# A one-core decode step: four order changes, compression weights loaded at once, and pinned loads

## The chip, the cores and the metric

The kernel runs on one core of one Trainium2 chip. The metric is device time in microseconds of one execution, as the median of several runs; lower is better. PE is the matmul engine (PEld its weight loads), DVE the vector engine, ACT the scalar engine, POOL the third elementwise engine, which also issues the gathers, and SP the engine whose queue issues most DMA transfers.

## The reference

One layer of a decoder step for a prompt of 1024 new tokens and 8 sample tokens that stand behind 2048 cached ones. D = 1024, 8 heads of 64, 2 key/value heads.

```python
h = rms_norm(x, norm_g)
proj = h @ w_in              # b, c gates, conv input, z_conv, q, kv (3 branches), gate logits, z_attn
q, k: rms_norm per head, rope
kv_cmp = compress_blocks(kv, cmp_pe, cmp_w)   # einsum('bcrjgd,rjde->bcjge'), blocks of 32 rows
o = gate0 * attn(q, kv_cmp) + gate1 * attn(q, top-16 blocks of 64) + gate2 * attn(q, last 512)
conv = short_conv(b * conv_in) * c
mix = concat(conv * silu(z_conv), o * silu(z_attn))
y = x + mix @ w_out
```

For the sample tokens the compressed branch covers the paged cache: its rows are gathered by the page table and multiplied by the compression weights cmp_w. All values are float32.

## The kernel before

Every large product is made of three matmuls on a high and a low part of each operand (h*h, l*h, h*l): a `copy` on ACT rounds a tile to its high part (L78), and a `sub` on DVE or POOL (L82) makes the low part. Each such pair of a copy and a subtraction stands between a tile's arrival and the matmuls that read it.

The program is written as Python generators, "streams". `merge` (L31) takes from the stream that is behind by its own costs; a stream says with `yield c` that it issued work of cost c. A tile framework then reorders the instructions of each engine by its own cost model, unless `keep` (keep_in_program_order) or `issue_after` binds them. Each engine carries out its own list in order, so an instruction that waits holds up all behind it on that engine.

The first merge runs `phase0` (norm, key/value rows, queries) beside the channel products. The second runs `first` (attention, then `out_stream`, the output projection by tiles of 128 tokens and 512 columns) beside `second` (convolution, `prefetch`, `early_out`, `cmp_stream`, `sample_stream`). The stages that the change touches:

- `kv_tile` and the compression of the prompt's rows: for pairs of key/value tiles, `token_pairs` (L427) loads rows across into `pr` with four DMAs, and `cmp_transposes` (L435, matmuls at L440) turns them. It is posted some steps later, as given at L657.
- The queries: `q_tile` runs twice with two sets of weights. The second set's four pieces are fetched by `w_loader`'s `fetch` (L169, DMA L171) and split by `split` (ACT L78, then POOL or DVE L82) between the tiles (L783 to L788). `tok_mm` does the products (L210 to L212), and `norm_rope` (L256) normalises and rotates the queries (DVE L267 to L277).
- `prefetch` (L1542) loads eight w_out pieces, which an earlier stage has split into DRAM (`wo_d`), fetches the compression weights cmp_w for the sample in four pieces (`cw_fetch`, L447; four DMAs each, L454) into one room, each with a copy and a subtraction, and issues the first two gathers of cached rows (`gather`, L1124, DMA L1127; two rooms `raw`). `early_out` (L1593) makes two output tiles early, while the attention ends.
- `cmp_stream` (L1131) has 16 units n. Each takes one gathered tile, regroups it with four copies (`regroup`, L1135, two on ACT and two on POOL), turns four pairs by PE (L1149), splits each into xh and xl, and multiplies by the compression weights (`product`, L1170), CD pairs behind. Its output goes into accs. `out_stream` runs beside it, at L1582 to L1588.
- `sample_stream` (L1301) does the sample's attention. The state rows `sdw`, `sd` come by SP (L1238), the gathered rows by POOL. In `values` (L1438), p is turned, `ptz` gets its high part from ACT and its low part from DVE, and the matmuls `o<-vhl,ptz` (L1466) follow. At the end, for two halves h, the sums are scaled (L1504 to L1514) and turned (L1515, `ptx`); from them come `mS` and the sample's own output rows (L1617).

```python
if rows is not None and t < 8:      # L656
    posts.append((lambda pr=token_pairs(rows, t - 1), t=t: cmp_transposes(pr, t - 1), 4 if t < 5 else 3 if t < 7 else 1))
if t in (3, 4, 5):                  # L787
    nxt[2](t - 2, ACT, EL)
raw = wpool.tile([128, 4, 2, 64], F32, name="cwr", tag="wx" if wpool is wk else "cwr")         # L449
r = rawp.tile([128, 2048], F32, name="raw", bufs=2)                                            # L1126
```

## Time and profile before

| what | value |
|---|---|
| median of 3 runs | 920.47 us (914.07 to 924.98) |
| the profiled execution, its own time | 922.36 us |
| span in its profile | 920.6 us |
| mean granted clock of PE | 0.978 |
| PE busy | 874.4 us, 95% |
| DVE, ACT, POOL busy | 63%, 58%, 44% |

The span goes from the first to the last instruction in the profile. An engine is busy while it carries out an instruction; a bracket behind a row of the timeline, as [2.33 <-DVE rb L275], says how long the engine stood idle just ahead and what it last waited for. PEclk is the share of the full 2.4 GHz that PE was granted.

### The profile page before, as it was taken

How to read it: one execution, taken by the hardware profiler on the slowest of the kernel's cores; microseconds unless marked ns; L12 is line 12 of the kernel's file. 1: busy time of each engine (PE TensorE's matmuls, PEld its weight loads, DVE VectorE, ACT ScalarE, POOL GpSimd, SP SyncE). 2: the span in 40 equal slices, each digit the busy share in tenths (PEclk: the TensorE clock that was granted, in tenths of full speed). 3: DMA queues.
4: the chain of work that ended last, by engine and by line, in shares of the span. 5: the costliest groups of instructions: out<-in, count | busy, mean ns of one | idle time of the engine just before them, and what ended most of it. 6: DMA issues, size and time to landing. Idle time of an engine off the chain costs nothing.

```text
span 920.6 us, 16583 instructions
## 1 busy us (share of the span) xinstructions
PE 874.4 (95%) x5769; PEld 784.8 (85%) x5769; DVE 576.8 (63%) x1482; ACT 532.7 (58%) x1350; POOL 400.5 (44%) x547
## 2 busy tenths in 40 slices
PE   8998999999899999999989999999989999999987
PEld 6898999989789889899979898999878788677765
DVE  5865627776555555765685677657745555765663
ACT  5552425433665655666565755666756776777761
POOL 4231303111454444544353543444654444677751
PEclk9998989989899999999999999999989999999999
DMA  7432402620011001220111000000977552667611
GB/s 261 127 96 71 120 10 77 223 80 21 16 30 36 24 24 46 70 69 13 59 58 24 24 12 13 24 1 7 274 263 270 198 193 94 239 214 245 221 67 48
DMA packets 67154, 91.14 MB, mean 99 GB/s; under 512 B 19191, under 2 KB 49343, under 8 KB 64894
## 3 DMA queue, kind: packets, MB, share of 16 engines
q1 hardware_dynamic: 58428, 52.16, 18.5%
q0 software_dynamic: 8064, 37.75, 12.3%
q8 instruction: 46, 0.75, 0.3%
q14 instruction: 38, 0.31, 0.1%
q10 hardware_dynamic: 578, 0.17, 0.1%
HBM read 77.92 MB, written 15.29 MB: 101 GB/s over the span
## 4 chain that ended last, share of the span: by engine, by line
PE 47%; ACT 7%; DVE 7%; issue 3%; POOL 3%; DMA 2%; SPq 0%; ACTq 0%; DVEq 0%; POOLq 0%
PE o L1024 7%; PE pt L1014 5%; PE s L940 5%; PE mm L227 5%; PE mm L225 5%; PE mm L226 5%; POOL P L989 2%; PE om L1170 2%; ACT P L930 1%; PE mm L1582 1%; PE mm L1583 1%; PE o L1466 1%; PE mm L1584 1%; PE pt L1149 1%; ACT ph L78 1%
## 5 line engine op out<-in xcount | busy, mean ns | idle before, releaser
L225 PE MATMUL mm<-hH,wh 128*128 128x384 f32 (+1 forms) x480 | 157.6, 328 | 2.3 <-ACT mixC L397 1.3
L227 PE MATMUL mm<-hH,wl 128*128 128x384 f32 (+1 forms) x480 | 154.9, 323 | 0.1
L226 PE MATMUL mm<-hL,wh 128*128 128x384 f32 (+1 forms) x480 | 154.6, 322 | 0.0
L82 POOL TENSOR_TENSOR wl<-wraw,wh 128x256 fp32r<-128x256 f32 (+1 forms) x105 | 78.1, 761 | 142.2 <-ACT wh L78 119.2
L930 ACT ACTIVATE P<-P,stat 128x640 f32<-128x640 f32 (+7 forms) x192 | 113.0, 590 | 38.1 <-DVE stat L928 37.5
L82 DVE TENSOR_TENSOR pl<-pt,ph 128x512 fp32r<-128x512 f32 (+1 forms) x164 | 102.8, 636 | 50.6 <-ACT ph L78 49.3
L78 ACT ACTIVATE ph<-pt 128x512 fp32r<-128x512 f32 (+1 forms) x164 | 88.4, 548 | 68.9 <-PE pt L1014 68.1
L989 POOL TENSOR_SCALAR P<-P,stat,gates 128x640 f32<-128x640 f32 (+7 forms) x128 | 100.3, 793 | 55.2 <-DVE stat L980 52.1
L1014 PE MATMUL pt<-ident,P 128*128 128x128 f32 x592 | 95.3, 279 | 6.1 <-POOL P L989 3.7
L940 PE MATMUL s<-k,q 128*128 128x320 f32 (+8 forms) x416 | 95.8, 333 | 1.9 <-DVE stat L928 1.9
L210 PE MATMUL mm<-wh,hH 128*128 128x256 f32 (+1 forms) x320 | 95.6, 299 | 1.3 <-ACT hH L78 0.7
L211 PE MATMUL mm<-wl,hH 128*128 128x256 f32 (+1 forms) x320 | 95.2, 297 | 1.7 <-DVE wl L82 0.9
L212 PE MATMUL mm<-wh,hL 128*128 128x256 f32 (+1 forms) x320 | 94.9, 296 | 1.2 <-DVE hL L82 1.2
L225 PEld LDWEIGHTS mm<-hH,wh 128*128 128x128 f32 x480 | 91.0, 190 | 3.3 <-ACT mixC L397 1.5
L227 PEld LDWEIGHTS mm<-hH,wl 128*128 128x128 f32 x480 | 91.3, 190 | 0.5 <-POOL wl L82 0.5
L226 PEld LDWEIGHTS mm<-hL,wh 128*128 128x128 f32 x480 | 91.3, 190 | 0.2
L928 DVE CUSTOM_DVE_ANT_0 P<-s,mask 128x32 f32<-128x32 f32 (+8 forms) x160 | 70.8, 473 | 26.2 <-PE s L940 22.3
L1014 PEld LDWEIGHTS pt<-ident,P 128*128 128x128 f32 x592 | 70.3, 140 | 19.3 <-POOL P L989 10.2
L1024 PE MATMUL o<-ph,v 128*128 128x256 f32 x264 | 74.5, 301 | 2.2 <-ACT ph L78 1.6
L1024 PE MATMUL o<-pl,v 128*128 128x256 f32 x264 | 73.4, 300 | 1.6 <-DVE pl L82 1.5
L940 PEld LDWEIGHTS s<-k,q 128*128 128x128 f32 x416 | 66.5, 190 | 6.1 <-PE pt L1014 1.6
L210 PEld LDWEIGHTS mm<-wh,hH 128*128 128x128 f32 x320 | 64.4, 201 | 2.4 <-ACT hH L78 1.4
(385 smaller groups left out, 2064.9 us busy)
## 6 DMA issues: line engine op xcount, KB each, us to landing
wraw<-in_w_in_dram SPq DMA_DIRECT2D x54, 256.0 KB
wo<-wo_d POOLq DMA_DIRECT2D x8, 512.0 KB, 5.7
out_s_win_dram<-in_state_win_kv_dram SPq DMA_DIRECT2D x8, 511.0 KB
xr<-in_x_prompt_dram SPq DMA_DIRECT2D x14, 256.0 KB
out_y_prompt_dram<-xr SPq DMA_DIRECT2D x14, 256.0 KB
sd<-in_state_win_kv_dram SPq DMA_DIRECT2D x5, 512.0 KB
mixA<-in_x_prompt_dram SPq DMA_DIRECT2D x4, 512.0 KB
xt<-in_x_prompt_dram SPq DMA_DIRECT2D x4, 512.0 KB
```

What stands on the lines that cost most here:

```text
L78: return ACT.activation(out, in_, AF.Copy)
L82: return eng.tensor_tensor(out, a, b, OP.subtract)
L210: PE.matmul(o[:, :n], hH[t // 3][:, k, s], wh, start=k == 0, stop=False)
L211: PE.matmul(o[:, :n], hH[t // 3][:, k, s], wl, start=False, stop=False)
L225: PE.matmul(o[:, :n], wh, hH[c][:, k], start=k == 0, stop=False)
L226: PE.matmul(o[:, :n], wh, hL[c][:, k], start=False, stop=False)
L227: PE.matmul(o[:, :n], wl, hH[c][:, k], start=False, stop=k == 7)
L930: return lambda: ACT.activation(P, P, AF.Exp, bias=stt[:, 0, c:c + 1], scale=-1.0, accum_out=stt[:, 1, c:c + 1])
L940: PE.matmul(s[:, a:b], q[:, i], k, start=first, stop=not first)
L989: POOL.tensor_scalar(P[:, i, :n], P[:, i, :n], stt[:, 2, c + i:c + i + 1], gates[:, qi, gt:gt + 1], op0=OP.mult, op1=OP.mult)
L1014: PE.transpose(p[:, y * 256 + i * 128:y * 256 + i * 128 + 128], src[:, i], ident)
L1024: PE.matmul(o[0][:, :256], v, X[:, y * 256:y * 256 + 256], start=br == 1 and x == 0 and y == 0 and X is h[0], stop=last and y + 1 == len(p ...
```

## The change

- A: the transposes of the last pair of tokens are posted two steps later instead of one.
- B: the fourth piece of the second query weights is fetched at t = 5 into one of two rooms named `rows`, and split at t = 7; before it went into a `wraw` room at t = 2 and was split at t = 5.
- C: the four pieces of cmp_w for the sample are fetched all at once into one tile that takes one of the two `raw` rooms; their copies stand among the steps of the early output tiles, in program order on ACT. The first gather is issued in `prefetch`, the second behind the fourth copy.
- D: the products run three pairs behind instead of two; regroup of the next unit comes half a unit later; the steps of `sample_start` are bound behind what was issued before them on ACT, DVE and POOL.
- E: the first half's end, `ends(0)`, is issued after the last low half of ptz.
- The second four w_out pieces (k of 4 and above) keep program order on SP and ACT; loads of state rows are issued after the store of the latest output tile.

```diff
+    def behind(*engines):
+        traced = nc.cur_bb.bb.instructions
+        with ExitStack() as st:
+            for e in engines:
+                st.enter_context(tc.issue_after(next(i for i in reversed(traced) if i.engine == e.engine)))
+            yield
...
-                r = home.tile([128, kp, n], F32, name=name, bufs=raw_bufs if name == "wraw" else 1)
+                if name == "rows":
+                    r = home.tile([128, 512], F32, name=name, bufs=ROWS).rearrange("p (k n) -> p k n", k=kp)
+                else:
+                    r = home.tile([128, kp, n], F32, name=name, bufs=raw_bufs if name == "wraw" else 1)
...
-            copy(ACT, h, raw)
+            r = copy(ACT, h, raw)
+            if not early:
+                keep(r)
...
-                posts.append((lambda pr=token_pairs(rows, t - 1), t=t: cmp_transposes(pr, t - 1), 4 if t < 5 else 3 if t < 7 else 1))
+                posts.append((lambda pr=token_pairs(rows, t - 1), t=t: cmp_transposes(pr, t - 1), 4 if t < 5 else 3 if t < 7 else 2))
...
+                    if t == 5:
+                        nxt[1](3, wk, "rows")
                     if t == 2:
                         nxt[2](0, ACT, EL)
-                        nxt[1](3)
-                    if t in (3, 4, 5):
-                        nxt[2](t - 2, ACT, EL)
+                    if t in (3, 4, 7):
+                        nxt[2]({3: 1, 4: 2, 7: 3}[t], ACT, EL)
...
-    CD = 2
+    CD = 3
...
-            if n + 1 < 16:
-                regroup(n + 1)
             if n in (4, 7, 10):
-                next(start, None)
+                with behind(ACT, DVE, POOL):
+                    next(start, None)
...
             for j in range(2):
+                if j and n + 1 < 16:
+                    regroup(n + 1)
...
-            SP.dma_start(r, state_win[b].rearrange("(p s) c -> p (s c)", s=4))
+            with tc.issue_after(stored[0].ins):
+                SP.dma_start(r, state_win[b].rearrange("(p s) c -> p (s c)", s=4))
...
-            sub(DVE, pz[:, :, 4:32:9, :], pv, f(pz[:, :, 0:28:9, :]))
+            last[0] = sub(DVE, pz[:, :, 4:32:9, :], pv, f(pz[:, :, 0:28:9, :]))
...
-        for h in range(2):
+        def ends(h):
...
+        with tc.issue_after(last[0].ins):
+            ends(0)
+        ends(1)
...
-        SP.dma_start(r, w_out[:, k, n * 512:(n + 1) * 512])
+        d = SP.dma_start(r, w_out[:, k, n * 512:(n + 1) * 512])
+        if k >= 4:
+            keep(d)
...
-            copy(ACT, w[:, 0], r)
+            c = copy(ACT, w[:, 0], r)
+            if k >= 4:
+                keep(c)
...
-        late = None
+        raw = rawp.tile([128, 4, 4, 2, 64], F32, name="raw", bufs=2)
+        for i in range(4):
+            cw_late.append(cw_fetch(raw[:, i], i))
...
-            if k % 2 == 0:
-                if late:
-                    late(cw2)
-                late = cw_fetch(rawp, k // 2)
             yield PREF
-        for i in range(2):
-            gather(i)
-            yield PREF
-        late(cw2)
-        yield 0
+        gather(0)
+        yield PREF
...
+        o = 0
         for t, homes in enumerate((("20", "00", "01", "10", "11"), ("11", "21", "00", "01", "10"))):
             homes = [f"q{i}" for i in homes]
-            yield from out_tile(0, t, lambda name, dt: qkv.tile([128, 512], dt, name=homes.pop(0)))
+            for c in out_tile(0, t, lambda name, dt: qkv.tile([128, 512], dt, name=homes.pop(0))):
+                yield c
+                if c and (t or o):
+                    cw_late.pop(0)(cw2)
+                o = c
+        cw_late.pop(0)(cw2)
+        gather(1)
```

The lines of the changed kernel are shifted: L78 is L88 there, L82 is L92, L1587 is L1615.

On DVE, in the query stage (B), the list before reads as follows; wl is the low half of a weight piece, from the room that stands behind the arrow, kd a piece of w_out that is split into DRAM, and q, qn, rs, ss, rb belong to the norm and the rotation of a query tile.

```order
L267 TENSOR_REDUCE ss<-rb 128x8
L82 TENSOR_TENSOR wl<-wraw,wh 128x256 x2
L82 TENSOR_TENSOR wl<-wx,wh 128x256
L196 RECIPROCAL rs<-rs 128x8
L197 SCALAR_TENSOR_TENSOR rs<-ss,rs 128x8
L198 SCALAR_TENSOR_TENSOR rs<-rs 128x8
L82 TENSOR_TENSOR kd_2784<-kd_2784,kd_2828 128x512
L199 SCALAR_TENSOR_TENSOR rs<-rs 128x8
L270 TENSOR_TENSOR qn<-q_1587,rs 128x512
L271 TENSOR_TENSOR q_1587<-qn,mixC 128x512
L275 TENSOR_TENSOR rb<-qn,mixC 128x8x32 x2
L82 TENSOR_TENSOR wl<-wraw,wh 128x256
```

And the same place now:

```order
L280 TENSOR_REDUCE ss<-rb 128x8
L92 TENSOR_TENSOR kd_2784<-kd_2784,kd_2828 128x512
L92 TENSOR_TENSOR wl<-wraw,wh 128x256 x2
L209 RECIPROCAL rs<-rs 128x8
L210 SCALAR_TENSOR_TENSOR rs<-ss,rs 128x8
L211 SCALAR_TENSOR_TENSOR rs<-rs 128x8
L92 TENSOR_TENSOR wl<-wx,wh 128x256
L212 SCALAR_TENSOR_TENSOR rs<-rs 128x8
L283 TENSOR_TENSOR qn<-q_1587,rs 128x512
L92 TENSOR_TENSOR wl<-rows,wh 128x256
L284 TENSOR_TENSOR q_1587<-qn,mixC 128x512
L288 TENSOR_TENSOR rb<-qn,mixC 128x8x32 x2
```

The low half of the fourth piece stood behind both products of the rotation and now stands ahead of them.

On ACT, from the end of the attention into the compressed branch (C), before; cw is a piece of the compression weights, ph a high half of the attention's, ot its sum, reg a regrouped gathered tile, xh a high half for `product`, mh one for an output tile:

```order
L78 ACTIVATE q_8574<-mixA 128x512
L78 ACTIVATE ph<-pt 128x512
L78 ACTIVATE cw_8302<-cwr 128x8x64
L78 ACTIVATE ph<-pt 128x512 x4
L78 ACTIVATE cw_8302<-cwr 128x8x64
L78 ACTIVATE ot<-o 64x128 x2
L78 ACTIVATE reg<-raw 128x8x64 x4
L78 ACTIVATE cw_8302<-cwr 128x8x64
L78 ACTIVATE xh<-pt 128x512
L78 ACTIVATE xh<-ptx 128x512
L78 ACTIVATE xh<-pt 128x512
```

And now:

```order
L88 ACTIVATE q_8563<-mixA 128x512
L88 ACTIVATE ph<-pt 128x512 x2
L88 ACTIVATE cw_8302<-raw 128x8x64 x2
L88 ACTIVATE ph<-pt 128x512 x2
L88 ACTIVATE cw_8302<-raw 128x8x64
L88 ACTIVATE ph<-pt 128x512 x3
L88 ACTIVATE ot<-o 64x128 x2
L88 ACTIVATE cw_8302<-raw 128x8x64
L88 ACTIVATE reg<-raw 128x8x64 x2
L88 ACTIVATE xh<-pt 128x512
L88 ACTIVATE xh<-ptx 128x512
L88 ACTIVATE xh<-pt 128x512
```

The four weight copies moved ahead of the first regroup, and only two regroup copies, those of the first unit, stand ahead of the first xh.

On DVE, at the end of the sample stage (E), before; acc and fac are sums and their scales, srows the scaled rows, xr an output tile:

```order
L1479 SCALAR_TENSOR_TENSOR acc<-acc,fac,o 64x256
L1504 TENSOR_SCALAR stats<-stats 32x1
L82 TENSOR_TENSOR vhl<-sdw,vhl 128x4x128
L1505 RECIPROCAL stats<-stats 32x1
L1510 SCALAR_TENSOR_TENSOR acc<-acc,fac 64x256
L1511 TENSOR_TENSOR acc<-acc,q_s 32x256
L1512 TENSOR_TENSOR srows_11279<-acc 64x128
L1587 TENSOR_TENSOR xr<-om,xr 128x512
L82 TENSOR_TENSOR ptz_9970<-pt,ptz_9970 128x4x4x8
L1514 TENSOR_TENSOR srows_11280<-srows_11280,srows_11279 32x128
L1479 SCALAR_TENSOR_TENSOR acc<-acc,fac,o 64x256
```

And now:

```order
L1501 SCALAR_TENSOR_TENSOR acc<-acc,fac,o 64x256
L1526 TENSOR_SCALAR stats<-stats 32x1
L92 TENSOR_TENSOR vhl<-sdw,vhl 128x4x128
L1527 RECIPROCAL stats<-stats 32x1
L1615 TENSOR_TENSOR xr<-om,xr 128x512
L92 TENSOR_TENSOR ptz_9967<-pt,ptz_9967 128x4x4x8
L1526 TENSOR_SCALAR stats<-stats 32x1 x2
L1527 RECIPROCAL stats<-stats 32x1 x2
L1531 TENSOR_SCALAR acc<-acc,fac 64x256
L1532 SCALAR_TENSOR_TENSOR acc<-acc,fac 64x256
L1533 TENSOR_TENSOR acc<-acc,q_s 32x256
L1501 SCALAR_TENSOR_TENSOR acc<-acc,fac,o 64x256
```

The low half of ptz stood behind the scaling of the first half and now stands ahead of it.

## Rows read from the trace of the kernel before

**Rows 1.** The page, busy time of each engine, share of the span and instructions.
```profile
PE 874.4 (95%) x5769; PEld 784.8 (85%) x5769; DVE 576.8 (63%) x1482; ACT 532.7 (58%) x1350; POOL 400.5 (44%) x547
```

**Rows 2.** Windows: us, busy PE, PEld, DVE, ACT, POOL, PEclk, DMA share, GB/s.
```profile
194.20:201.00 6.80, 6.14 (x28) 6.14 (x29) 5.34 (x13) 1.49 (x4) 0.00 (x0) 0.50 0.00 0
464.00:474.00 10.00, 8.21 (x53) 7.52 (x52) 8.59 (x22) 5.37 (x12) 3.82 (x6) 1.00 0.33 105
678.90:685.70 6.80, 6.22 (x25) 5.63 (x26) 2.99 (x5) 3.95 (x9) 4.75 (x6) 0.50 0.97 368
686.00:790.00 104.00, 99.94 (x658) 85.76 (x657) 57.01 (x110) 70.79 (x144) 50.35 (x62) 1.00 0.56 192
790.00:895.00 105.00, 100.16 (x591) 74.94 (x590) 72.12 (x145) 77.41 (x177) 74.67 (x65) 1.00 0.62 206
897.70:900.70 3.00, 3.00 (x15) 3.00 (x16) 0.08 (x1) 0.00 (x0) 0.00 (x0) 0.50 0.27 102
911.00:918.00 7.00, 5.58 (x24) 4.15 (x23) 2.05 (x3) 0.00 (x0) 0.00 (x0) 1.00 0.04 7
```

**Rows 3.** Timeline around 69 us: start, length, engine, line, operation, idle before.
```profile
67.18 2.60 SPq L432 DMA_DIRECT2D pr<-rows  x4
...
71.35 1.09 PE L440 MATMUL tp<-ident,pr 128*128 128x128 f32 x4 [2.33 <-DVE rb L275]
```

**Rows 4.** Timeline of the query stage, 191 to 195 us.
```profile
191.66 0.72 ACT L78 ACTIVATE wh<-wraw 128x256 fp32r<-128x256 f32 x2 [1.10 <-DMA wraw<-in_w_in_dram]
...
192.12 0.39 PE L210 MATMUL mm<-wh,hH 128*128 128x256 f32 x1 [0.51 <-ACT wh L78]
...
192.70 1.10 DVE L271 TENSOR_TENSOR q<-qn,mixC 128x512 f32<-128x512 f32 x1
...
193.31 0.39 PE L211 MATMUL mm<-wl,hH 128*128 128x256 f32 x1 [0.80 <-POOL wl L82]
...
193.72 0.75 DVE L275 TENSOR_TENSOR rb<-qn,mixC 128x256 f32<-128x256 f32 x2
...
194.86 0.58 PE L211 MATMUL mm<-wl,hH 128*128 128x256 f32 x1 [0.94 <-DVE wl L82]
```

**Rows 5.** Timeline from the attention's end into the compressed branch.
```profile
672.12 0.63 ACT L78 ACTIVATE cw<-cwr 128x512 fp32r<-128x512 f32 x1 [4.02 <-DMA cwr<-in_cmp_w_dram]
...
673.36 2.19 ACT L78 ACTIVATE reg<-raw 128x512 f32<-128x512 f32 x4
...
677.98 0.63 ACT L78 ACTIVATE cw<-cwr 128x512 fp32r<-128x512 f32 x1 [2.42 <-DMA cwr<-in_cmp_w_dram]
...
679.14 0.58 PE L1170 MATMUL om<-xh,cw 128*128 128x256 f32 x1 [2.49 <-ACT xh L78]
...
685.76 0.47 PE L1584 MATMUL mm<-wo,ml 128*128 128x512 f32 x1
```

**Rows 6.** Timeline of the sample stage's end.
```profile
893.65 1.43 DVE L1510 SCALAR_TENSOR_TENSOR acc<-acc,fac 64x256 f32<-64x256 f32 x1
...
894.75 1.44 POOL L82 TENSOR_TENSOR ml<-mixA,mh 128x512 fp32r<-128x512 f32 x1
895.11 1.36 DVE L1511 TENSOR_TENSOR acc<-acc,q_s 32x256 f32<-32x256 f32 x1
...
897.64 3.47 PE L1466 MATMUL o<-vhl,ptz 128*64 128x256 f32 x16 [2.54 <-DVE ptz L82]
...
902.35 0.48 DVE L1510 SCALAR_TENSOR_TENSOR acc<-acc,fac 64x256 f32<-64x256 f32 x1 [0.73 <-ACT fac L1507]
```

**Rows 7.** Timeline: a store of an output tile, and the first reader of a state tile.
```profile
749.89 0.34 SPq L1588 DMA_DIRECT2D out_y_prompt_dram<-xr  x1
...
785.92 0.47 PEld L1320 LDWEIGHTS pt<-ident,sdw 128*128 128x128 f32 x4
```

**Rows 8.** PE's waits from 686 to 790 us (line, releaser: us, times, longest), and the gathers of L1127.
```profile
PE om L1170 <- DVE xl L82: 1.3, 4, 0.3
...
DMA to landing us min/median/max: 5.5/5.9/9.0
```

More of the change, by code (lines that the diff above doesn't have):

```diff
@@ L1 @@
-from contextlib import ExitStack
+from contextlib import ExitStack, contextmanager
 from functools import partial
@@ L64, in hymba_step_kernel @@
     WARM = 8
+    ROWS = 2
     keep = tc.keep_in_program_order
+    @contextmanager
+    def behind(*engines):
[4 more added lines that the diff above has]
+            yield
     PE, ACT, DVE, POOL, SP = nc.tensor, nc.scalar, nc.vector, nc.gpsimd, nc.sync
@@ L354, in hymba_step_kernel @@
     rope0 = mCf[:, 0:1152].rearrange("p (i t d) -> p i t d", i=2, t=NT)
-    ROWS, ENDS = 2, 14000
+    ENDS = 14000
     wk.tile([128, 512], F32, name="rows", bufs=ROWS)
@@ L445, in hymba_step_kernel, with cw_fetch @@
     cmpw = io["cmp_w"]
-    def cw_fetch(wpool, i):
-        raw = wpool.tile([128, 4, 2, 64], F32, name="cwr", tag="wx" if wpool is wk else "cwr")
+    def cw_fetch(raw, i):
+        early = raw is wk
+        if early:
+            raw = wk.tile([128, 4, 2, 64], F32, name="cwr", tag="wx")
         for r in range(2):
@@ L1436, in weigh @@
             return Sb
+        last = [None]
         def values(c, h, Sb):
@@ L1551, in prefetch @@
             wo[0, k] = w[:, 0], w[:, 1]
-            if k % 2 == 0:
-                if late:
-                    late(cw2)
-                late = cw_fetch(rawp, k // 2)
             yield PREF
-        for i in range(2):
-            gather(i)
-            yield PREF
-        late(cw2)
-        yield 0
+        gather(0)
+        yield PREF
+    cw_late = []
     begun = set()
+    stored = [None]
     def out_tile(n, t, room, made=None):
@@ L1587, in out_tile @@
         DVE.tensor_tensor(xr, o, xr, OP.add)
-        SP.dma_start(y_prompt[s, cols], xr)
+        stored[0] = SP.dma_start(y_prompt[s, cols], xr)
         if made:
```

## The prediction

> **What bounds the kernel now.** I read the page's busy times first, then the windows, then the timelines around PE's idle gaps, then the waits. The reader is to see in the first that PE is the bound: busy 874.4 of 920.6 us [rows 1], so PE's idle time is 46.2 us, and a microsecond on any other engine counts only where PE waits for it. The second loss is the clock. The profiled execution has a mean granted clock of 0.978, and in the windows there are stretches at 0.50, which is 1.2 GHz instead of 2.4 [rows 2]: behind a stall of PE in the query stage (194.2 to 201), in the stage of the compressed branch (678.9 to 685.7) and at the end (897.7 to 900.7). In such a stretch PE looks busy, yet what it does takes twice the time. So a stall costs itself and, where the clock falls, up to the length of the slow stretch halved. That the clock need not fall shows in 464 to 474: PE is idle 10 - 8.21 = 1.79 us there, and all of it runs at 1.00 [rows 2].
>
> All sums below are made against the profiled execution, 922.36 us (span 920.6 and 1.8 around it). That is 1.9 above the median of the runs shown, and I take 1.9 off at the end.
>
> **A, transposes of the last pair of tokens, posted one step later.** PE stands 2.33 us before L440 [rows 3]. The profile names a DVE operation as releaser, but that result is not read there; the four loads of pr that L440 reads were issued from 67.18 over 2.60 us, and they are the late part [rows 3]. The change moves six small matmuls in front of that wait and takes none of it away: the same loads, issued at the same place. Were each as long as one of the four of L440 (1.09 / 4 = 0.27 us), six would fill 1.6 us; they are of 8 to 12 columns, so I take -0.5, an estimate, and keep -1.6 and 0 as ends.
>
> **B, fourth piece of the second query weights fetched earlier, into a room of its own.** Before, ACT reached that piece's copy and waited 1.10 us for the load; PE then stood 0.51 us for the copy, 0.80 for POOL's low half and 0.94 for DVE's, 2.25 us together [rows 4]. The last of these is not a late input: DVE had the 1.10 us product of L271 and the two of L275, 0.75 us together, ahead of it, 1.85 us [rows 4]. In the new order DVE's low half stands ahead of L271, ACT's copies no longer wait for a load, and the load goes out some stages earlier. Of 2.25 us I let 0.55 stand, since the copy and the two low halves still follow one another: -1.7. The slow stretch behind the stall lasted 6.8 us [rows 2]; at full clock the same work takes 3.4 less. Ends: -5.65 (all of both) and 0 (the wait is only moved).
>
> **C, the sample's compression weights fetched at once.** Before, their four pieces took turns in one room, each load waiting for the piece before it: ACT stood 4.02 us for a piece at 672.12 and 2.42 us for the last at 677.98, and behind that last copy, in order on ACT, stood the xh copy for which PE waited 2.49 us at 679.14 [rows 5]. Then 6.8 us ran at 0.50 [rows 2]. Now the 16 loads go out back to back before the output tiles, so ACT's copies find them landed. A price stands against this: the raw tile of the weights holds one of the two gather rooms, so the second gather starts only behind the fourth copy, and on POOL behind a regroup copy. ACT was free at 668.1 (4.02 before 672.12); I allow 3.5 us for the copies of ot and of the weights (0.6 each), the sums on DVE and POOL and that regroup copy, and have the gather issued at 671.6. With the median landing of 5.9 us [rows 8] its data are there at 677.5; two regroup copies of 0.55 us (2.19 over 4 [rows 5]) end near 678.6. PE meanwhile has the first unit's products, which no longer wait. So PE goes on at about 678.6 with the second unit. What it did from 678.9 to 685.7 in 6.22 us at half clock [rows 2] is 3.1 at full clock, so the row of output matmuls that starts at 685.76 [rows 5] starts near 681.7: -4.0. The ends: -4.8, if the gather is another 0.8 us earlier; +2.5, if it takes the longest landing, 9.0 us [rows 8], 3.1 more than the median, and the clock falls behind that stall on dense matmuls as before (3.4): -4.0 + 3.1 + 3.4.
>
> **D, products three pairs behind, regroup half a unit later.** From 686 to 790 PE is idle 104 - 99.94 = 4.06 us [rows 2]. The largest part is four waits of L1170 for the xl half, 1.3 us together [rows 8]; a third pair in flight is meant for just these. Regroup half a unit later puts four copies of 0.55 in another place on ACT and POOL, where ACT works 70.8 and POOL 50.4 of 104 us [rows 2], so they have room. I take -0.9, two thirds of the 1.3; ends -2 (half of the idle time) and +2 (the same, as new waits).
>
> **E, the end of the sample stage: `ends(0)` behind the last ptz.** Before, DVE did L1510 for 1.43 us and L1511 for 1.36 us in front of the low half of ptz, for which PE stood 2.54 us [rows 6]; the 16 matmuls behind it took 3.47 us, at half clock [rows 2, 6]. In the new order ptz stands ahead of all of `ends(0)`, so it is ready near 895.1, when PE ends the matmuls in front: -2.54. If the clock stays, the 16 take 1.7 less. What is late next: the final chain of DVE and ACT operations to both ptx transposes now has 9 and 5 output matmuls as cover in place of 13 and 6, and 5 more stand in front of L1617. An output matmul goes by every 0.23 us (24 in 5.58 [rows 2]), so 5 cover 1.2 us, less than the chain's copy, sum and transposition. I add 0.95 us of new waits: -3.3. Ends: -4.3 and 0.
>
> DVE's L1510 took 1.43 us while POOL's 1.44 us ml ran for most of it, and another of the same shape later took 0.48 with POOL idle [rows 6]. The Trainium skill, "GPSIMD Engine Reference", section "1. Specifications", says that POOL shares its interfaces to SBUF with VectorE and contends with DVE instructions that read two operands there; the trace agrees. By that rule E would give only -1.4, if ml still ran beside the moved L1510 and L1511 and they held up the first ptx (1.43 and 1.36 instead of about 0.45 each, 1.9 more).
>
> **The pinned ones.** The second four w_out pieces keep program order on SP and ACT; the state tiles' loads go behind the store issued at 749.89, and the first reader of one stands at 785.92 [rows 7], 36 us later, four times the longest gather landing. I cost both at 0; what hides them is that distance. Bounds: -1 (less traffic beside the gathers at 680) and +3 (a load late by a third of 9.0 us).
>
> **Sum**: -0.5 - 1.7 - 3.4 - 4.0 - 0.9 - 3.3 = -13.8; 922.36 - 13.8 = 908.6, and less 1.9 for the median 906.7. All ends to the good give -19.4 (901.1), all to the bad +7.5 (928.0).
>
> **Rivals.**
> R1, the clock falls all the same. Stalls shrink but do not vanish at 192 and 895, and the slow stretches stay. For it: the stall at 71 is hardly touched, and new waits come near 900. Against it: 1.79 us of idle within 464 to 474 left the clock at 1.00 [rows 2]. Then 3.4 and 1.7 are not won: 906.7 + 5.1 = 911.8. The Trainium skill, "TensorE: Matmul & The Clock Gate", section "What's actually happening", says that the throttled state is the default, which activity releases, and that the monitor runs free of the kernel; by that rule the same stall may or may not cost its slow stretch from run to run, which gives this rival its 911.8 in some runs. The trace has a stall of each kind: 2.49 us with a slow stretch behind it, 1.79 without [rows 2, 5].
> R2, the second gather is late. Its issue now hangs on the fourth copy, and gathers have landed in 9.0 us [rows 8]; C turns from -4.0 to +2.5: 906.7 + 6.5 = 913.2. Against it: 5.9 is the median of 16.
> R3, slower. Regroup half a unit later: if the four copies come too late for the next unit, PE waits in each of 15 units. A unit lasts 104 / 15 = 6.9 us, half of it 3.5; two copies take 1.1 us on each engine, and with three copies of 0.63 queued ahead on ACT it is 3.0. If ACT is behind by 1.8 us more, PE waits up to 1.8 per unit, 26 us together: 906.7 + 26 = 933. This outweighs the other gains from 0.9 us per unit (13.8 / 15). For it: PE is the bound and regroup is in its path. Against it: ACT is idle a third of this stage [rows 2].
> R4, the change does not carry through. The sample stage (790 to 895) has PE idle for 4.84 us [rows 2] and waits for loads and copies; were it paced by its loads, A to D (-0.5 - 5.1 - 4.0 - 0.9 = -10.5) would be given back there: 917.2. Against it: gathers and state loads stand on no large wait there.
>
> **How the numbers follow.** Forecast 0.57; R1 0.18, R2 0.12, R4 0.08, R3 0.05. A measurement of this kernel can tell about 1% from no change, which is 911.3 and 929.7. The forecast's own range is 902 to 912, nine tenths of it below 911.3 (0.51); of R1 I count 0.07, of R2 0.03 and of R4 0.01 as faster: 0.62. Slower: 0.04 of R3 and 0.01 of R4, 0.05; the rest, 0.33, is within 1%. Range: the low end is 900, under the sum of all good ends, for the scatter of the runs; the high end is 917, which holds R1 and R2 and half of R4.
>
> **What would show it.** B: no slow stretch behind 194 and no DMA wait of ACT there. C: no wait of ACT for the weights, the second gather landed by 677.5, the long row of output matmuls some 4 us earlier. D: the four waits of L1170 for xl gone, idle time from there to the end of the stage under 4. E: PE's matmuls on ptz without a wait, at full clock. I am wrong if PE waits for reg copies in most units, if the slow stretches stand where they were, or if the sample stage is longer by what was saved ahead of it.

## The result and the profile after

The changed kernel took 907.65 us (median of 4 runs, 904.77 to 911.45), the kernel before 921.01 beside it (4 runs, 914.07 to 924.98): a ratio of 0.9854 with the 95% interval 0.9809 to 0.9898. The prediction was 906.7 with 900 to 917. The same kernel run again later, as one of the experiments, took 912.24 (6 runs) at a ratio of 0.9915 (0.9884 to 0.9947). Both say faster, by 13 us in the first set of runs and 8 to 9 in the second. The profiled execution took 911.45, so its own time is the slowest of its four.

The page of the changed kernel, its first row (compare [rows 1]):

```profile
PE 865.2 (95%) x5769; PEld 776.3 (85%) x5769; DVE 580.0 (64%) x1482; ACT 531.6 (58%) x1350; POOL 403.0 (44%) x547
```

PE has the same 5769 matmuls, and its share is the same 95%: 9.2 us less busy, 1.7 less idle. Nearly all that was gained looks like faster matmuls, and that is the clock, as the windows show (same columns as [rows 2]):

```profile
72.00:78.80 6.80, 6.47 (x55) 6.50 (x56) 4.00 (x7) 1.94 (x4) 2.92 (x2) 1.00 0.30 86
188.00:201.00 13.00, 12.41 (x96) 11.90 (x96) 10.47 (x25) 4.81 (x10) 0.88 (x2) 1.00 0.28 102
464.00:467.40 3.40, 3.40 (x16) 3.21 (x15) 2.48 (x7) 1.86 (x5) 1.03 (x2) 0.50 0.20 77
678.30:690.00 11.70, 9.43 (x56) 8.09 (x56) 3.84 (x7) 7.35 (x14) 8.94 (x10) 1.00 0.72 249
888.50:892.00 3.50, 3.30 (x20) 2.57 (x18) 2.76 (x8) 1.61 (x5) 0.16 (x1) 1.00 0.21 76
```

The slow stretches behind 194, 679 and 898 of [rows 2] are gone, and with them one near 71, which the prediction's list left out; in the kernel before it reads:

```profile
71.30:78.10 6.80, 6.75 (x30) 6.43 (x31) 2.97 (x6) 1.12 (x2) 2.58 (x2) 0.50 0.27 74
```

A new one stands at 464, behind a wait that the change does not touch.

To see where the time went I took the start of certain matmuls of PE, counted from the first one in the trace (their number is the same, and outside a few places their order too), and subtracted the kernel before. One row is one profiled execution; a column is the difference over that stretch in us. The letters say which part lies in it; 257 to 650 is attention, which no part touches.

```
us of before            0-61   A 61-89  89-185  B 185-207  207-257  257-650  C,D,pins 650-790  790-885  E 885-914
changed                +1.00    -3.88   +0.04     -4.31     +3.10    +1.77        -5.82          +0.72     -3.52
changed again          -0.31    -3.90    0.00     -4.80     +1.96    +1.46        -3.64          +0.64     -3.53
A undone               -0.17    +0.01   -0.01     -4.04     +3.29    +2.79        -3.65          +0.63     -3.55
B undone               +0.04    -3.90   -1.56     +0.15     -0.53    +0.32        -5.84          +0.64     -3.58
E undone               +1.92    -3.89   +0.06     -3.84     +2.58    -0.14        -4.77          +0.65     +0.07
D undone               -0.84    -3.59   +0.02     -4.24     +3.05    +1.52        -0.33          +0.24     -3.54
two pairs              +1.00    -3.88   -1.61     -4.73     +3.15    +2.89        +1.40          +0.24     -3.53
regroup early          +1.06    -3.87   -1.61     -4.38     +3.29    +1.83        -4.58          +0.63     -3.51
two pairs, C undone    +1.72    -3.87   +0.04     -4.87     +3.27    +2.03        -1.33          +0.23     -3.52
no pins                -0.24    -3.88   -1.58     -5.40     +3.20    -0.07        -1.09          +0.63     -3.58
no w_out pin           +2.20    -3.86   +0.02     -4.39     +3.15    +1.73        -5.16          +0.65     -3.51
no pins, low on POOL   -0.68    -3.88   -0.01     -4.37     +3.17    +1.69        +3.24          +0.61     -3.54
weights' low on POOL   -0.23    -3.90    0.00     -4.33     +1.81    +1.45        -6.78          +0.64     -3.55
```

The reader is to see how sharp this is where the medians are not. A and E stand at the same value, within 0.3, in every kernel that has them and at 0.0 to 0.1 in the one that has not. The first 61 us and the stretch 89 to 185 scatter by 3.0 and 1.6 us with no regard to any part. Of the stretch 650 to 790 a share is clock: half the length of the slow stretches that lie in it, taken from the records of the granted clock. It is 3.4 us in before, changed again, A undone, two pairs and no pins; 1.7 in E undone and "two pairs, C undone"; 5.1 in "no pins, low on POOL"; none in the others. "Without clock" below means that a kernel's own share is taken off its figure. The 3.4 of the kernel before stay in, so such figures compare the versions with each other; against the kernel before with its share off too, each is 3.4 higher (-2.4 and -3.6 for the two executions of the changed kernel).

The rows of the changed kernel for A and B, a timeline (compare [rows 3, 4]):

```profile
72.33 0.63 PE L453 MATMUL tp<-ident,pr 128*128 128x128 f32 x4 [1.48 <-DVE qn L283]
...
187.21 0.71 ACT L88 ACTIVATE wh<-rows 128x256 fp32r<-128x256 f32 x2
...
189.30 0.38 PE L224 MATMUL mm<-wl,hH 128*128 128x256 f32 x1 [0.43 <-DVE wl L92]
...
190.44 0.39 PE L224 MATMUL mm<-wl,hH 128*128 128x256 f32 x1 [0.17 <-DVE wl L92]
...
219.79 0.63 ACT L279 ACTIVATE rb<-q 128x512 f32<-128x512 f32 x1 [2.33 <-DVE q L290]
...
220.78 0.45 PE L238 MATMUL mm<-hH,wh 128*128 128x384 f32 x1 [1.04 <-ACT wh L88]
```

ACT's copy of the fourth piece waits for no load, and 2.25 us of waits at PE have become 0.60 (0.43 and 0.17). But 30 us later ACT stands 2.33 us for DVE's rotation of a query tile, with a weight copy queued behind it, and PE waits 1.04 for that copy.

For C, the timeline from the end of the attention (compare [rows 5]):

```profile
659.07 1.73 POOL L1007 TENSOR_SCALAR P<-P,stat,gates 128x640 f32<-128x640 f32 x2
...
659.91 0.63 ACT L88 ACTIVATE cw<-raw 128x512 fp32r<-128x512 f32 x1 [0.44 <-DMA raw<-in_cmp_w_dram]
...
660.78 1.27 POOL L92 TENSOR_TENSOR q<-mixC,q 128x512 fp32r<-128x512 f32 x1
...
663.31 0.63 ACT L88 ACTIVATE cw<-raw 128x512 fp32r<-128x512 f32 x1 [1.80 <-DMA raw<-in_cmp_w_dram]
663.86 0.39 PE L1042 MATMUL o<-pl,v 128*128 128x256 f32 x1 [1.94 <-DVE pl L92]
...
673.02 1.03 POOL L1145 DMA_INDIRECT raw<-in_cache_cmp_kv_dram,idx_c  x1 [0.17 <-issue]
...
680.29 0.66 PE L1167 MATMUL ptx<-ident,reg 128*128 128x128 f32 x4 [1.99 <-ACT reg L88]
```

And the low halves of the weight pieces on DVE, from the view of that tile (shortest, median and longest in ns, and when):

```profile
L92 DVE TENSOR_TENSOR cw<-raw,cw x4: 677/686/2901, 659.7 to 671.3; 128x512 fp32r<-128x512 f32 x4
```

The wait of 2.49 us at [rows 5] is gone, but two others have come: 1.94 us at 662, where PE stands for a low half pl that is queued on DVE behind the first weight piece, an operation of 2.90 us where the median is 0.69; and 1.99 us at 680, for the regroup copy of the second gather, which was issued at 673.02.

### The profile page after: what moved, and what is told of

Read it like the earlier page. It is cut to its first block, busy times and chain, and to the rows that moved or that the text cites. A ratio compares the mean times of both kernels' runs of the same rounds, so it can differ in the third digit from the quotient of the medians.

```text
span 909.7 us, 16568 instructions
## 1 busy us (share of the span) xinstructions
PE 865.2 (95%) x5769; PEld 776.3 (85%) x5769; DVE 580.0 (64%) x1482; ACT 531.6 (58%) x1350; POOL 403.0 (44%) x547
## 4 chain that ended last, share of the span: by engine, by line
PE 48%; ACT 7%; DVE 6%; issue 3%; POOL 3%; DMA 2%; SPq 1%; POOLq 0%; ACTq 0%; DVEq 0%
PE o L1042 7%; PE pt L1032 5%; PE mm L240 5%; PE mm L239 5%; PE s L958 5%; PE mm L238 5%; PE om L1188 3%; PE pt L1167 2%; POOL P L1007 2%; DMA raw<-in_cmp_w_dram 1%; PE mm L1612 1%; PE mm L1610 1%; PE mm L1611 1%; ACT P L948 1%; PE s L1358 1%
## 5 line engine op out<-in xcount | busy, mean ns | idle before, releaser
L92 POOL TENSOR_TENSOR wl<-wraw,wh 128x256 fp32r<-128x256 f32 (+1 forms) x104 | 77.0, 758 | 141.1 <-ACT wh L88 129.0
L92 DVE TENSOR_TENSOR pl<-pt,ph 128x512 fp32r<-128x512 f32 (+1 forms) x164 | 102.6, 636 | 49.6 <-ACT ph L88 48.3
L88 ACT ACTIVATE ph<-pt 128x512 fp32r<-128x512 f32 (+1 forms) x164 | 88.1, 548 | 70.1 <-PE pt L1032 69.4
L225 PE MATMUL mm<-wh,hL 128*128 128x256 f32 (+1 forms) x320 | 92.8, 290 | 1.6 <-DVE hL L92 1.6
L223 PE MATMUL mm<-wh,hH 128*128 128x256 f32 (+1 forms) x320 | 93.5, 292 | 0.1
L224 PE MATMUL mm<-wl,hH 128*128 128x256 f32 (+1 forms) x320 | 92.8, 290 | 0.6 <-DVE wl L92 0.6
L225 PEld LDWEIGHTS mm<-wh,hL 128*128 128x128 f32 x320 | 62.1, 194 | 2.0 <-DVE hL L92 2.0
```

The source lines that it names most:

```text
L92: return eng.tensor_tensor(out, a, b, OP.subtract)
L223: PE.matmul(o[:, :n], hH[t // 3][:, k, s], wh, start=k == 0, stop=False)
L224: PE.matmul(o[:, :n], hH[t // 3][:, k, s], wl, start=False, stop=False)
L225: PE.matmul(o[:, :n], hL[t // 3][:, k, s], wh, start=False, stop=k == 7)
```

## The experiments

All undo or alter one thing in the changed kernel. Times are medians, each with its ratio to the kernel before on the same chip; the interval of such a ratio is about 0.003 either way, 3 us. Since the parts are worth 1 to 6 us, each verdict rests on the place in the trace and on the table above, and the ratio stands beside it. It says little: with A, B, E or the pins undone the ratios (0.9897 to 0.9920) do not stand apart from the changed kernel's two (0.9854 and 0.9915).

A second measure does not hang on one execution. Every run has its span and its mean granted clock, and the one times the other is about what the run would have taken at full clock; the rest is what the clock cost. Here is the mean of each version less that of the kernel before on the same chip, in us, with an interval of about 1.5 either way:

```
changed again -5.2    A undone -4.5       B undone -6.2          E undone -3.3               D undone -0.1
two pairs -0.9        regroup early -3.6  no pins -2.0           no w_out pin -1.3
two pairs, C undone -3.1                  no pins, low on POOL 0.0   weights' low on POOL -6.5
```

The clock cost 15 to 17 us a run before, 8.4 and 11.7 in the two sets of the changed kernel, 12.9 with A undone, 10.9 with E undone. So about half of the gain is clock. Of the other half E gives some 2 us and the pins 3; A and B stand within the interval of nothing; and with D undone it is all gone.

**E undone.**

```diff
-        with tc.issue_after(last[0].ins):
-            ends(0)
+        ends(0)
```

> The changed kernel with part E undone: the first half's end is no longer bound behind the last low half of ptz. Place-by-place theory: the wait of 2.5 us ahead of the 16 matmuls on ptz and the slow stretch come back, 3.5 us more, 911.2. Chance theory: the wait alone, 1.8 net of new waits that go, 909.5. If the scheduler does by itself what the binding asks for, no difference.

912.83 us, ratio 0.9910 (0.9875 to 0.9945). The timeline shows what stood in [rows 6], the wait of 2.54 us to a hundredth:

```profile
886.22 1.43 DVE L1532 SCALAR_TENSOR_TENSOR acc<-acc,fac 64x256 f32<-64x256 f32 x1
887.69 1.37 DVE L1533 TENSOR_TENSOR acc<-acc,q_s 32x256 f32<-32x256 f32 x1
...
890.23 3.03 PE L1488 MATMUL o<-vhl,ptz 128*64 128x256 f32 x16 [2.54 <-DVE ptz L92]
```

In the changed kernel the same place reads:

```profile
886.85 0.27 DVE L92 TENSOR_TENSOR ptz<-pt,ptz 128x128 fp32r<-128x128 f32 x1
...
887.56 2.03 PE L1488 MATMUL o<-vhl,ptz 128*64 128x256 f32 x16
...
889.02 0.48 DVE L1532 SCALAR_TENSOR_TENSOR acc<-acc,fac 64x256 f32<-64x256 f32 x1
...
892.10 1.29 POOL L92 TENSOR_TENSOR ml<-mixC,mh 128x512 fp32r<-128x512 f32 x1 [3.44 <-ACT mh L88]
892.11 1.43 DVE L1534 TENSOR_TENSOR srows<-acc 64x128 f32<-64x128 f32 x1
...
894.25 0.24 PE L1537 MATMUL ptx<-ident,srows 32*128 32x32 f32 x1 [0.78 <-DVE srows L1536]
```

The wait and its slow stretch are E's: 3.59 us between -3.52 and +0.07. The slow stretch stands there in both executions without E and in none of the 12 with it. The place-by-place theory holds here. At full clock E is worth 1.9 us over all runs (-3.3 against -5.2), which fits the place; its 1.7 of clock is too small to show in the runs' clock.

**A undone.**

```diff
-4 if t < 5 else 3 if t < 7 else 2))
+4 if t < 5 else 3 if t < 7 else 1))
```

> The changed kernel with part A undone: the transposes of the last pair are posted one step later again instead of two. Place-by-place theory (what the two profiles differ by at a place is what the part there is worth): PE's wait ahead of the transposes is 2.3 us again instead of 1.45 and the slow stretch behind it at 71 is back, so about 3.9 us more than the changed kernel, 911.5. Chance theory (which slow stretches an execution has is not set by the change): only the wait's 0.9 us comes back, 908.5, and the profile may or may not have the slow stretch.

912.86 us, ratio 0.9918 (0.9895 to 0.9941). The row of the wait and the window behind it:

```profile
71.18 0.79 PE L453 MATMUL tp<-ident,pr 128*128 128x128 f32 x4 [2.33 <-DVE rb L288]
```

```profile
71.50:78.30 6.80, 6.80 (x32) 6.46 (x31) 2.60 (x6) 1.12 (x2) 2.22 (x2) 0.50 0.27 65
```

Six small matmuls moved ahead cut the wait from 2.33 to 1.48, and the slow stretch behind it is there in both executions without them and in none of the 12 with them. So in the traces A is worth 3.9 us, 3.4 of it the clock, and the chance theory falls at this place. The runs agree as far as they can: at full clock A is worth 0.7, and the clock cost 12.9 us with A undone against 10.4, the mean of the changed kernel's ten runs. Their ratio alone (0.9918 against 0.9854 and 0.9915) would not show it.

**B undone.**

```diff
-                    if t == 5:
-                        nxt[1](3, wk, "rows")
                     if t == 2:
                         nxt[2](0, ACT, EL)
-                    if t in (3, 4, 7):
-                        nxt[2]({3: 1, 4: 2, 7: 3}[t], ACT, EL)
+                        nxt[1](3)
+                    if t in (3, 4, 5):
+                        nxt[2](t - 2, ACT, EL)
```

> The changed kernel with part B undone: the fourth query weight piece fetched at t = 2 into the old room and split at t = 5. Theory that B's gain is mostly given back: of 4.3 us won by 201 us, 3.1 are lost again by 246, since the norm and rotation of the last query tiles on ACT and DVE then come too late; so about 1.2 us more than the changed kernel, 909. Rival, that the loss up to 246 has nothing to do with B: 4.3 more, 912. The profile tells them apart: with B undone, is PE's wait of 1.04 us for a weight copy at 219.7 still there?

910.52 us, ratio 0.9897 (0.9860 to 0.9935). PE's waits come back:

```profile
188.13 0.39 PE L223 MATMUL mm<-wh,hH 128*128 128x256 f32 x1 [0.90 <-ACT wh L88]
189.26 0.39 PE L224 MATMUL mm<-wl,hH 128*128 128x256 f32 x1 [0.74 <-POOL wl L92]
190.82 0.39 PE L224 MATMUL mm<-wl,hH 128*128 128x256 f32 x1 [0.94 <-DVE wl L92]
```

Locally B is worth 4.5 us (-4.31 against +0.15), but a loss of 1.8 to 3.3 in the next stretch is there in every kernel with B and not in this one (-0.53), nor is the wait of 1.04. Where PE comes earlier, DVE's rotations of the last query tiles are late; the wait of 1.04 is part of that loss, and the rest was not traced. Over both stretches B is worth 0.8 us by the first execution of the changed kernel (-1.21 against -0.38) and 2.5 by the second (-2.84). The runs at full clock do not confirm even that (-6.2 without B, -5.2 with it): as a whole B is not shown to gain.

**The pins, both taken away.**

```diff
-        if k >= 4:
-            keep(d)
...
-            if k >= 4:
-                keep(c)
...
-            with tc.issue_after(stored[0].ins):
-                SP.dma_start(r, state_win[b].rearrange("(p s) c -> p (s c)", s=4))
+            SP.dma_start(r, state_win[b].rearrange("(p s) c -> p (s c)", s=4))
```

> The changed kernel without the pins: the second four w_out pieces and their copies no longer keep program order, and the state tiles' loads are not bound behind a store. As predicted: no difference, 907.7 within 1. Rival, that the loads' absence beside the gathers is what shortens the compressed branch (690 to 790 was 4 us shorter than before, where 0.9 was forecast): 3 us more, 910.7, with the loss between 680 and 790.

913.20 us, ratio 0.9920 (0.9894 to 0.9947). The loss lies from 681 to 701, and the timeline shows it:

```profile
681.40 2.23 DVE L92 TENSOR_TENSOR wo<-wor,wo 128x512 fp32r<-128x512 f32 x1 [2.40 <-ACT wo L88]
...
681.78 1.29 POOL L92 TENSOR_TENSOR ml<-mixC,mh 128x512 fp32r<-128x512 f32 x1
...
684.16 3.29 DVE L92 TENSOR_TENSOR wo<-wor,wo 128x512 fp32r<-128x512 f32 x1
...
684.51 1.28 POOL L92 TENSOR_TENSOR ml<-mixA,mh 128x512 fp32r<-128x512 f32 x1
...
688.10 0.66 PE L1167 MATMUL pt<-ident,reg 128*128 128x128 f32 x4 [2.45 <-DVE xl L92]
```

Without the pin the pieces arrive early, their low halves stand on DVE among the compressed branch's, and two of them take 2.23 and 3.29 us; pinned, the four took 0.68 to 0.78. The xl behind them is late, PE stands 2.45 us and a slow stretch follows. With the clock's share taken off, the stretch 650 to 790 gives -4.5 here against -5.8 and -7.0 in the two executions of the changed kernel: 1.3 to 2.5 us, and 1.7 more for the slow stretch behind the wait. At full clock over all runs it is 3.2 (-2.0 against -5.2). My zero for the pins was wrong.

**Only the w_out pin taken away.**

```diff
-        if k >= 4:
-            keep(d)
...
-            if k >= 4:
-                keep(c)
```

> The changed kernel without the pin on the second four w_out pieces; the state tiles' loads stay bound. Without both pins PE waited 2.45 us at 685.6 and the stretch 681 to 701 lost 4.3 us. If it is the pieces' low halves on DVE (2.23 and 3.29 us instead of 0.68, with the product's xl queued behind them): the wait and 3 to 4 us of loss are there. If it is the traffic of the state tiles' loads beside the gathers: no wait, no loss.

913.63 us, ratio 0.9899 (0.9859 to 0.9939).

```profile
689.77 2.20 DVE L92 TENSOR_TENSOR wo<-wor,wo 128x512 fp32r<-128x512 f32 x1
...
690.12 1.29 POOL L92 TENSOR_TENSOR ml<-mixA,mh 128x512 fp32r<-128x512 f32 x1
...
692.63 0.66 PE L1167 MATMUL pt<-ident,reg 128*128 128x128 f32 x4 [1.34 <-DVE xl L92]
```

The long low halves and the wait are there without any state load near, so it is the pieces; but the wait is half as long (1.34), and 0.7 to 1.8 us are lost over the stretch, not 3 to 4. What the other half was, the state loads' traffic or chance, this trace leaves open. The runs at full clock (-1.3 here, -2.0 without both pins) leave nothing for the state loads' binding, within 1.5 us: it is the w_out pin that counts.

**Both pins away, the low halves of those pieces on POOL.**

```diff
-        def split(el=DVE):
+        def split(el=POOL):
```

> The changed kernel without both pins, as e6_no_pins, but with the low halves of the second w_out pieces on POOL instead of DVE: loads as early, traffic the same, only the engine differs. Theory that DVE is held beside POOL while it reads two operands from SBUF: PE's wait of 2.45 us and the loss of 4.3 us from 681 to 701 are gone, or 1 us of it stays for POOL's longer list. Rival, that the gathers land late for the traffic (8.0 and 9.2 us there against 5.7): the wait and the loss stay.

920.12 us, ratio 0.9989 (0.9962 to 1.0016): all of the gain lost. At the place in question the timeline says:

```profile
686.96 1.31 POOL L92 TENSOR_TENSOR ml<-mixA,mh 128x512 fp32r<-128x512 f32 x1
687.00 0.69 DVE L92 TENSOR_TENSOR xl<-pt,xh 128x512 fp32r<-128x512 f32 x1 [0.38 <-ACT xh L88]
...
698.82 0.63 ACT L88 ACTIVATE wo<-wor 128x512 fp32r<-128x512 f32 x1 [5.64 <-DMA wor<-in_w_out_dram]
...
700.81 1.09 PE L1167 MATMUL pt<-ident,reg 128*128 128x128 f32 x4 [5.05 <-POOL wo L92]
```

The wait of 2.45 us is gone, as the theory of a held DVE said. What neither theory said: POOL's list is now longer, the pieces' room comes free later, ACT stands 5.64 us for the next piece with the xh copies behind it, and PE stands 5.05. Of the traffic as a cause nothing is left at the first place; as a whole the version is of no use.

**The compression weights' low halves on POOL.**

```diff
-            sub(EC, cw[:, i * 4:i * 4 + 4, :, 64:128], raw, f(h))
+            sub(EC if early else POOL, cw[:, i * 4:i * 4 + 4, :, 64:128], raw, f(h))
```

> The changed kernel with the low halves of the sample's four compression weight pieces made on POOL instead of DVE. Theory that DVE is held beside POOL: the first of these on DVE took 2.90 us while POOL worked, against 0.68 for the others, and PE stood 1.94 us at 662 for a low half queued behind it; on POOL it holds nobody, the wait goes, 1.9 us less than the changed kernel, 905.7. Rival, that the late loads of the pieces are the cause (ACT waited 0.44 and 1.80 us for them with attention copies behind): PE's wait stays above 1.5 us and the time is the same.

910.75 us, ratio 0.9908 (0.9874 to 0.9943), not told apart from the changed kernel beside it (912.24, 0.9915). PE's waits from 650 to 675 are two short ones (line, releaser: us, times, longest); below them the longest of the changed kernel from 650 to 690:

```profile
PE o L1042 <- ACT ph L88: 0.5, 1, 0.5
PE om L1188 <- ACT xh L88: 0.4, 1, 0.4
```

```profile
PE ptx L1167 <- ACT reg L88: 2.0, 1, 2.0
PE o L1042 <- DVE pl L92: 1.9, 1, 1.9
```

The 1.94 is gone, though ACT still waited 0.40 and 2.11 us for the loads. So DVE's long operation was the cause of that wait, and the loads were not. The 1.9 us expected of it do not show: without clock the stretch stands at -6.8, between -5.8 and -7.0 of the changed kernel's two executions. Part of why is in the second of these, where the weight copies fell elsewhere and PE waited 0.9 and 0.7 us there instead of 1.94.

**D undone.**

```diff
-    CD = 3
+    CD = 2
...
+            if n + 1 < 16:
+                regroup(n + 1)
             if n in (4, 7, 10):
-                with behind(ACT, DVE, POOL):
-                    next(start, None)
+                next(start, None)
...
-                if j and n + 1 < 16:
-                    regroup(n + 1)
```

> The changed kernel with part D undone: two pairs behind, regroup at the start of a unit, sample start steps unbound. As predicted: 0.9 us more, 908.5. Place-by-place theory, by which 690 to 790 is shorter by 4 us through D alone: 4 more, 911.7. Theory that the pins made most of that: 1 more or less.

916.30 us, ratio 0.9952 (0.9932 to 0.9973), 4.1 us beside the changed kernel's 912.24, the largest loss of any part undone. PE's waits from 690 to 790, first row:

```profile
PE om L1188 <- DVE xl L92: 2.4, 5, 1.2
```

Without clock -0.3 against -5.8 and -7.0: with the other parts in place D is worth 5.5 to 6.7 us, not 0.9. That is more than the stage gained. From 686 to 790, where the kernel before has no slow stretch, as many matmuls (656) take 4.3 and 4.6 us less in the changed kernel and 1.6 more with D undone: part of D's worth makes good what the other parts cost there.

**Two pairs behind, the rest of D kept.**

```diff
-    CD = 3
+    CD = 2
```

> The changed kernel with two pairs behind instead of three, the rest of D kept. If the third pair is what D gives: the four waits of PE for xl in the compressed branch (1.3 us before) are back and the time is 1 to 4 us more than the changed kernel. If the later regroup is what D gives: no difference.

914.48 us, ratio 0.9923 (0.9894 to 0.9952).

```profile
PE om L1188 <- DVE xl L92: 2.2, 3, 1.6
```

The waits for xl are back; three pairs have none, as PE's longest waits of the changed kernel from 690 to 783 show:

```profile
PE ptx L1208 <- DVE kcs L1200: 1.4, 2, 1.0
PE pt L1208 <- DVE kcs L1200: 0.7, 2, 0.4
```

With 3.4 of clock taken off +1.40, the stretch stands at -2.0 against -5.8: the third pair is worth 3.8 us or more, and by the runs at full clock 4.3 (-0.9 against -5.2). The binding of the `sample_start` steps, the rest of D, was never undone alone.

**Three pairs, regroup early.**

```diff
+            if n + 1 < 16:
+                regroup(n + 1)
             if n in (4, 7, 10):
...
-                if j and n + 1 < 16:
-                    regroup(n + 1)
```

> The changed kernel with three pairs behind, but regroup at the start of a unit again. With D undone the stage from 690 to 790 lost 5.6 us, with two pairs alone 7.1 (1.7 of it a slow stretch): so the third pair seems to be what D gives. Third-pair theory: no difference, within 1 us in that stage. Theory that the two need each other: 2 us or more lost there. PE waiting for reg copies in the changed kernel (my slower rival) would show as a gain here.

911.38 us, ratio 0.9876 (0.9843 to 0.9908). Over the stretch -4.58 against -5.82 and, without clock, -7.0: the late regroup gives 1 to 2 us (1.6 at full clock over the runs), and two executions of one kernel differ by as much. It costs nothing, so the slower rival is out.

**Two pairs, C undone.**

```diff
-        raw = rawp.tile([128, 4, 4, 2, 64], F32, name="raw", bufs=2)
-        for i in range(4):
-            cw_late.append(cw_fetch(raw[:, i], i))
+        late = None
...
+            if k % 2 == 0:
+                if late:
+                    late(cw2)
+                late = cw_fetch(rawp.tile([128, 4, 2, 64], F32, name="cwr", tag="cwr"), k // 2)
...
-        gather(0)
-        yield PREF
+        for i in range(2):
+            gather(i)
+            yield PREF
+        late(cw2)
...
-    CD = 3
+    CD = 2
```

> The changed kernel with part C undone (four pieces of the compression weights in one room in turn, both gathers in the prefetch) and two pairs behind: with three pairs the rooms of the old part C leave no space, so this is to be held against the changed kernel with two pairs (e9_two_pairs, 914.5). As predicted: C is worth 4.0 us, 918.5. Place-by-place theory: 660 to 690 was shorter by only about 1.2 us with C, since PE's wait at 662 took back what the earlier regroup gave: 915.7, with PE waiting again for an xh copy behind a weight copy, and no wait at 662.

909.60 us, ratio 0.9857 (0.9830 to 0.9884), to be held against two pairs with C: 0.9923 (0.9894 to 0.9952). Its longest wait of PE from 650 to 690; the others are 0.5 us or less:

```profile
PE om L1186 <- ACT xh L88: 2.5, 1, 2.5
```

The old wait of 2.49 is back, the new ones are not. Over the stretch, without clock, it stands at -3.0 against -2.0 with C. So C by itself gains nothing and may cost 1 us (2.2 by the runs at full clock, -3.1 against -0.9; 6 by the medians, which hold the chance of the clock too). This version, with neither C nor the third pair, runs as fast as the changed kernel by its median. What C gives is room: with the old weights' room beside the gather rooms the third pair's tiles have no space, as the expectation says; no run shows it, and what three pairs would give without C's cost is open.

**The changed kernel again.**

> The changed kernel once more, unaltered, for a firmer median and for the scatter of places that no part touches. Place-by-place theory: the same differences against the kernel before at A, B, E and from 690 to 790 as in the first profile; the 1.0 us lost in the first 60 us and the slow stretch at 464 are chance and need not return. Expected 907.5, within 904 to 911.

912.24 us, ratio 0.9915 (0.9884 to 0.9947), above what was expected. The same wait that stands at 680.29 above is here at 678.10, and the window behind it:

```profile
678.10 1.08 PE L1167 MATMUL ptx<-ident,reg 128*128 128x128 f32 x4 [2.01 <-ACT reg L88]
```

```profile
678.20:681.60 3.40, 3.40 (x15) 3.21 (x16) 2.20 (x4) 2.69 (x7) 2.47 (x2) 0.50 0.78 298
```

Same program, same wait (1.99 and 2.01), and the clock fell in one and held in the other. A gap of 1.79 us near 460 did so too: clock 1.00 behind it in before, 0.50 in the changed kernel.

## Why the prediction was right, and where it was not

The time was right (906.7 against 907.65, and 912.24 the second time) with a sum whose terms were partly wrong, one against the other, so that it came out so near is in good part luck. Against its own execution the forecast was -13.8; the two profiled executions gave -10.9 and -12.1. The clock adds to the luck: it cost 8.4 us a run in the set that was forecast and 11.7 in the second.

- **A, forecast -0.5, measured -3.9.** The step that failed is "takes none of it away": the wait was cut by 0.85, and the slow stretch behind it, worth 3.4, did not come. My list of slow stretches left out this one (71.3 to 78.1, above); R1 named the stall, but I gave its clock no price.
- **B, forecast -5.1, measured -4.3 to -4.8 at the place and +2.0 to +3.1 within the next 50 us.** Its local working held: 1.65 us of waits and the slow stretch went. What failed is that I followed the query stage only as far as the fourth piece. When a stall goes, the next engine in line must be asked too: here the norm and rotation on DVE, for which ACT had 2.33 us to stand. R4 had the mechanism, but put it in the sample stage.
- **C, forecast -4.0, measured about 0, or a loss of 1 to 2.** Of the 4.0, 3.1 was the slow stretch behind 679, which was gone in one execution of the changed kernel and there at half its length in the other. "ACT's copies find them landed" failed, with waits of 0.44 and 1.80; more costly was that the low half beside POOL took 2.90 us where I took 0.69. The second gather was issued at 673.02, not 671.6, and landed 6 us later, and PE stood 1.99 for it. R2 is in part what happened.
- **D, forecast -0.9, measured -5.5 or more.** The mechanism was right, its size off: I priced only the four waits that the view of waits lists (1.3 us), where the third pair took away 3.8 or more. The forecast end, -2, was half of PE's idle time there, and idle time hides most of it: the 656 matmuls from 686 to 790 take 4.3 us less at the same clock, but PE's idle time among them fell only from 4.06 to 2.67. The row of such a product matmul is 0.28 us long while the next can start 0.12 us after it, so PE counts as busy through a gap of up to 0.16.
- **E, forecast -3.3, measured -3.5**, with ptz ready before PE was, full clock, and one new wait of 0.78 ahead of the second ptx, where 0.95 was allowed. The sentence on the shared interfaces was right as well: L1532 took 0.48 with POOL idle and 1.43 beside it, and a small L1534 took 1.43 beside POOL's ml. E did not shrink to -1.4, because ml did not run beside the moved operations: L1532 started at 889.02 with POOL idle, and ml met only L1534, behind whose 1.43 us PE waited the 0.78.
- **The pins, forecast 0, measured 1.3 to 4.2.** I asked whether a load would be late, not what an early one lets loose on DVE.
- **R1** is true of some places and not of others. At 71 and 898 the slow stretch came with the wait and went with it in all executions. At 464 and near 679 it came in some executions and not in others with the same wait. The Trainium skill, "TensorE: Matmul & The Clock Gate", section "What's actually happening", has the monitor run free of the kernel; the two executions with 1.99 and 2.01 us agree.
- **R3** is out: among the waits from 690 to 783 none is for reg.

## What to carry to other kernels

Price a stall with the slow stretch behind it, and look at both in several executions before calling either a gain: here two thirds of what A and E gave in the traces (5.1 of 7.5 us) was clock. Multiply span and clock of every run before you believe a median: at full clock the runs of one version scatter by some 1.5 us, and E, the pins and D came apart. Follow a stage that is made earlier until another engine's queue ends the wait, for B lost half or more of its gain in the 50 us behind it. Do not size a gain by idle time alone: two thirds of what the stage from 686 to 790 gained had counted as busy. And ask of every operation that is pulled forward onto an in-order engine what stands behind it and what runs beside it; without two pins that looked idle, two of four subtractions fell into a moment where they took three to five times as long.

## What the runs showed of the hardware

A subtraction of 128x512 on DVE with both operands in SBUF (cw<-raw,cw and wo<-wor,wo) took 0.68 us with POOL idle. Where POOL was already at work when it began, on an operation or on issuing a gather, it took longer: 2.90, 2.23, 3.29 and 2.20 in the rows above, and 1.31 at 74.75 of the changed kernel, beside the second half of one operation. The first, second and fourth ended some 0.55 us after a POOL operation did (q at 662.05, ml at 683.07 and 691.41), while POOL's own hardly grew (1.27 for q, 1.28 and 1.29 for ml). A subtraction with an operand in PSUM (xl<-pt,xh) kept 0.69 right beside a POOL operation (687.00 above).

Not every meeting goes against DVE. In the changed kernel the fourth weight piece began just ahead of a POOL operation that takes 0.50 us on average:

```profile
671.28 0.69 DVE L92 TENSOR_TENSOR cw<-raw,cw 128x512 fp32r<-128x512 f32 x1
671.29 1.00 POOL L1057 TENSOR_TENSOR mixA<-ot,mixA 128x128 f32<-128x128 f32 x1 [3.16 <-DVE ot L1055]
```

Here DVE kept its time and POOL's was longer. The same shows at 759.81, where a low half of w_out took 0.78 us and POOL's ml beside it 1.74 instead of 1.29, though there POOL was at work on a copy when DVE began. So the operation that comes first mostly holds the other, but what decides in every case these runs do not show.

The Trainium skill, "GPSIMD Engine Reference", section "1. Specifications", says that POOL's interfaces to SBUF are shared with VectorE and that instructions of two SBUF inputs contend. The trace agrees, and adds the size: up to nearly 5 times as long for the DVE operation (3.29 against 0.68), twice as long for POOL's (1.00 against 0.50).
